# Latent tokens ordered by column in the neighbourhood attention, with scores for 416 keys instead of 512

## The chip, the cores and the metric

The kernel runs on one core of one Trainium2 chip. The metric is the device time of one execution in microseconds; the time of a kernel is the median of several runs. The core has TensorE (PE in the profile) with its weight loader (PEld), VectorE (DVE), ScalarE (ACT) and GpSimd (POOL); SyncE (SP) issues the transfers here.

## The reference, cut to what matters

Two layers of a backbone work on 256 latent and 256 context tokens of width 2048. Layer 0 mixes tokens by pooling, layer 1 by neighbourhood attention with 32 heads of 64; each is followed by a gated FFN of width 5504. Every sub-layer has an RMS norm, whose result is scaled and shifted by a modulation made from two vectors, one for each stream. The latent tokens are a grid of 4 rows and 64 columns. A latent query reads, in all 4 rows, the 16 columns around its own (clamped at the edges), with a learned bias by the distance in rows and columns, and beside these all 256 context keys:

```python
col_start = jnp.clip(col - kw // 2, 0, GRID_W - kw)
col_ok = (col[None, :] >= col_start[:, None]) & (col[None, :] < col_start[:, None] + kw)
...
s_loc = jnp.einsum('bhqd,bhkd->bhqk', q_r, k_band, preferred_element_type=f32) * scale + bias
s_loc = jnp.where(band_ok, s_loc, -jnp.inf)
s_ctx = jnp.einsum('bhqd,bhkd->bhqk', q_r, kc, preferred_element_type=f32) * scale
p = jax.nn.softmax(jnp.concatenate([s_loc, s_ctx], axis=-1), axis=-1).astype(v_band.dtype)
return (jnp.einsum('bhqk,bhkd->bhqd', p[..., :n_loc], v_band)
        + jnp.einsum('bhqk,bhkd->bhqd', p[..., n_loc:], vc))
```

## The kernel before, in words

Weights come from memory in pieces of 128 × 1024 fp32 (512 KB), loaded by `load` (L130) on SP. `split` makes two parts of each, a high one on ACT (L146) and a low one on DVE (L148), in a type that TensorE multiplies in one pass (f32r). A product of activations and weights is three products of parts: high with high, high with low, low with high. Tokens lie along the free side of a tile, features along the partitions.

The stages follow one another. Stage 0 makes the modulation of layer 0 on PE (`mod_pe`, tiles wm, products L182) and the pooling mixer (products pm, L563 to L565, with weights wp). FFN 0 follows; meanwhile DVE makes the modulation of layer 1, a piece at a time (`pair` and `single`, L242 to L265, tiles wm again), by a generator that the FFN's loop steps through. Then `normalise` makes the input of the attention: for each of 16 tiles of features and each stream one product on DVE (L401), the high part on ACT (L404) and the low part on DVE (L409), each 128 × 256, into the tile A. The attention is `_attention` (L1113 on): the first value products `_values` (L1108 to L1110), and then a pair of heads at a time. `kq_tile` makes keys of 512 tokens (L1173 to L1175) and queries of 256 (L1191, L1195); `rot` turns the latent ones by the rotary table rp (DVE L1146, L1148, L1149; POOL L1147). `attend` runs for the pair before, interleaved with `kq_tile` by `step`:

- `scores`, for each head and each block r of 128 queries: two products of 512 keys, those of the latent tokens first (L1221, L1222); the bias is added and the row's extreme found on DVE (L1231), the exponential on ACT (L1235), the scaling on DVE (L1236, L1237). The bias of a head is a strip of 128 × 384 (192 KB), loaded once a head (L1219) into the middle of a tile of zeros, and read at two places for the two blocks. A strip holds the bias of a query of one grid row for six grid rows, so one strip serves all grid rows by a shift.
- `turned`, for each head and block: four PE transposes of 128 × 128 (L1244) and one copy out of PSUM on DVE (L1245) into the tile pt.
- `finish`, for each pair: eight value products in plain fp32, four tiles of keys times two heads, 256 queries each (L1256), and a copy of the result on ACT (L1259).

A projection by wo (L1317), FFN 1 and the last norm follow.

Nobody writes the order of an engine's work out by hand: the program's scheduler places each instruction in the order of its engine by its own estimate of times, with a few calls for high priority. So a transfer that waits for nothing can stand much earlier in SP's queue than where the code calls for it. The transfers on SP take eight completion semaphores in turn, and each waits until the one eight places before it has landed.

Of the kernel before, what the change touches and what calls it, by code (L numbers as in the profile page):

```python
# [10 lines left out]
F32 = mybir.dt.float32  # L11
F32R = mybir.dt.float32r
AF = mybir.ActivationFunctionType
ALU = mybir.AluOpType
# [3 lines left out]
P = 128  # L18
D = 2048
KT = D // P  # L20
T = 256
F = 5504
NF = F // P
H = 32
W = 64
EPS = 1e-6
MASKED = -1.0e30
PAD = 8
POOL_WINDOWS = (2, 4, 8, 16)

# [28 lines left out]
def kernel(ctx: ExitStack, tc: tile.TileContext, xT, cxT, wmod, wg, wu, wd, wp,  # L59
                         wq, wv, wo, vec, cc, rope, inv, strips, out):  # L60
    nc = tc.nc
# [3 lines left out]
    ap0 = ctx.enter_context(tc.tile_pool(name="ap0", bufs=1))  # L65
# [27 lines left out]
    ident = main.tile([P, P], F32, name="ident")  # L93
# [5 lines left out]
    hl = main.tile([P, KT, T], F32, name="hl")  # L99
# [107 lines left out]
    def mod_pieces(pool):  # L207
# [28 lines left out]
        def pair(a):  # L236

            acc = sums_of(f"macc_{a}")
            for k in range(KT):
                w = staged(f"wm1_{a}_{k}").rearrange("p (c n) -> p c n", c=2)  # L240
                g, kk = divmod(k, 4)
                nc.sync.dma_start(w, wmod[1, a : a + 2, g, :, 512 * kk : 512 * kk + 512].rearrange("c p n -> p c n"))  # L242
                if k == 0:
                    nc.vector.tensor_scalar(acc, w, sc2[:, k, 0:1], None, op0=ALU.mult)
                else:
                    nc.vector.scalar_tensor_tensor(acc, w, sc2[:, k, 0:1], acc, op0=ALU.mult, op1=ALU.add)  # L246
                yield 1.0
            for c in range(2):
                fold(acc[:, c], a + c + 8, f"{a + c}")
# [75 lines left out]
    def M(l, which, k, s):  # L325
        return modT[l, which * 4 + k // 4][:, k % 4, s : s + 1]
# [66 lines left out]
    A = {}  # L393

    def normalise(l, which, h_of, streams, rstd, pool, ks=range(KT), keep=A):

        for k in ks:
            a = ap0.tile([P, 2, 2, T], F32R, tag=f"A{k}", name=f"A{k}_{l}_{which}")
            y = pool.tile([P, 2, T], F32, tag="t2", name=f"nrm{l}{which}{k}")
            for s in streams:  # L400
                nc.vector.scalar_tensor_tensor(y[:, s], h_of(s)[:, k, :], M(l, which + 1, k, s),  # L401
                                               rstd[s] if type(rstd) is list else rstd[:, T * s : T * s + T],
                                               op0=ALU.mult, op1=ALU.mult)
                nc.scalar.activation(a[:, 0, s, :], y[:, s], AF.Identity, bias=M(l, which, k, s))  # L404
# [4 lines left out]
                ins = nc.vector.scalar_tensor_tensor(a[:, 1, s, :], y[:, s], M(l, which, k, s),  # L409
                                                     a[:, 0, s, :].bitcast(F32), op0=ALU.add, op1=ALU.subtract)  # L410
            keep[k] = a
            if l == 1 and k == 1:
                hold[:] = [ins.ins]
# [2 lines left out]


    v_first = []
    with ExitStack() as ph0:
        p0 = ph0.enter_context(tc.tile_pool(name="p0", bufs=1, reuse_waits="tile"))  # L420
        f0 = ph0.enter_context(tc.tile_pool(name="f0", bufs=6, reuse_waits="tile"))
# [57 lines left out]
        with ExitStack() as phs:  # L479
# [19 lines left out]
            for j in range(2):  # L499
                t = st.tile([P, 2, WP], F32, bufs=1, name=f"pad{j}")  # L500
# [3 lines left out]
            for j in range(2):  # L504
                t = st.tile([P, 158], F32, bufs=1, name=f"sh{j}")
# [430 lines left out]

    tail = _attention(tc, ap0, bank, ld, A, M, hl, wq, wv, wo, rope, strips, ident, v_first)

    with ExitStack() as ph2:
        f1 = ph2.enter_context(tc.tile_pool(name="f1", bufs=8, reuse_waits="tile"))
# [140 lines left out]
        for j, (a, b) in enumerate(((0, 4), (4, 6), (6, 8), (8, 12), (12, 16))):  # L1083
            v = hl[:, a:b, :]
# [28 lines left out]
def _attention(tc, ap0, bank, ld, A, M, hl, wq, wv, wo, rope, strips, ident, v_first):  # L1113

    nc = tc.nc

# [6 lines left out]
    with ExitStack() as es:  # L1123
        op = es.enter_context(tc.tile_pool(name="op", bufs=1, reuse_waits="tile"))
        at = es.enter_context(tc.tile_pool(name="at", bufs=2, reuse_waits="tile"))
        rp = op.tile([P, 2, T], F32, name="rp")
        nc.sync.dma_start(rp, rope)

        sts = []
        for j in range(2):  # L1130
            t = op.tile([P, 10 * W], F32, name=f"strip{j}")
            nc.gpsimd.memset(t, 0.0)
            sts.append(t)

        qzs = []
        for j in range(2):
            t = op.tile([P, 2, T], F32R, name=f"qz{j}")
# [75 lines left out]
        def scores(m, b, r):  # L1213

            h = 2 * m + b
            ks, qd, qz = KEYS[m]
            strip = sts[b]
# [3 lines left out]
            nc.tensor.matmul(ps, qd[:, b, P * r : P * r + P], ks[:, b, :], start=True, stop=False)  # L1221
            nc.tensor.matmul(ps, qz[:, b, P * r : P * r + P], ks[:, b, :], start=False, stop=True)  # L1222
            if r == 0:
                bias = strip[:, 2 * W : 10 * W].rearrange("p (a t) -> p a t", a=2)
            else:
                a = strip[:, :]
                bias = bass.AP(a.tensor, a.offset, [a.ap[0], [6 * W, 2], [1, 4 * W]])

            sb = at.tile([P, 512], F32, tag="sb", bufs=3, name=f"sb{h}_{r}")
            nm = at.tile([P, 1], F32, tag="nm", name=f"nm{h}_{r}")  # L1230
            nc.vector.tensor_tensor_reduce(  # L1231
                out=sb.rearrange("p (a t) -> p a t", a=2), in0=ps.rearrange("p (a t) -> p a t", a=2),
                in1=bias, scale=-1.0, scalar=3.0e38, op0=ALU.add, op1=ALU.min, accum_out=nm)
# [3 lines left out]
            nc.vector.tensor_scalar(sb, sb, sm, None, op0=ALU.mult)  # L1237
            return sb, sm

        def turned(m, b, r, sb, pt):  # L1240

            pT = bank("d", f"pT{2 * m + b}_{r}")
            for j in range(4):
                nc.tensor.transpose(pT[:, P * j : P * j + P], sb[:, P * j : P * j + P], ident)  # L1244
            nc.vector.tensor_copy(pt[:, :, P * r : P * r + P], pT.rearrange("p (j q) -> p j q", j=4))  # L1245

        def attend(m, v, vc):

            pts = [None, None]

            def finish():
                po = bank("d", f"o{m}")
                for j in range(4):
                    for b in range(2):
                        c = vc + 64 * b
                        nc.tensor.matmul(po[64 * b : 64 * b + 64, :T], v[:, j, c : c + 64], pts[b][:, j, :],  # L1256
                                         start=(j == 0), stop=(j == 3), tile_position=(0, 64 * b))
                O[m] = op.tile([P, T], F32, name=f"O{m}")
                nc.scalar.copy(O[m], po[:, :T])  # L1259

            probs = {}
            for i in range(6):
                if i == 1 and ending:
                    ending.pop()()
                if 2 <= i:
                    b, r = divmod(i - 2, 2)
                    if r == 0:
                        pts[b] = at.tile([P, 4, T], F32, tag="pt", name=f"pt{2 * m + b}")
# [189 lines left out]
```

## Time and profile before

| | |
|---|---|
| runs | median 3055.77 us, 3055.04 to 3058.32, three runs |
| the profiled execution's own time | 3055.81 us |
| its span | 3054.0 us |
| mean granted clock of PE in it | 0.992 |
| instructions | 40391 |
| products and transposes on PE | 14846 |
| bytes moved | 568 MB, mean 186 GB/s |

Times in the profile count from the span's start. PE, DVE and so on stand ahead of a row's line number (L1244 is line 1244 of the kernel) and of its tile names (out<-in). A row with x8 holds eight instructions in a row. In a table of windows each engine has its busy time and its number of instructions, then come the clock that PE was granted, the share of time in which the 16 transfer engines were busy (a little over 1 when full), and GB/s. In the views of waits a row says which engine and line waited, for what, and then the total in us, the number of times and the longest. Products on PE overlap, so the pitch from start to start is what one costs.

### The profile page before, as it was taken

Reading aid. Unit: us, or ns where it says so; the run is one execution under the profiler, and the core shown is the slowest. Engines: PE = TensorE matmul, PEld = TensorE weight load, DVE = VectorE, ACT = ScalarE, POOL = GpSimd, SP = SyncE. Lnnn points to the kernel's source line nnn. Section 1 sums busy time; section 2 is a strip of 40 time slices with the busy share of each in tenths; the row PEclk is TensorE's granted clock in tenths of the full one; section 3 lists DMA queues with packets and bytes.
Section 4 is the critical chain, followed back from the end, with each engine's and each line's share of the span. In section 5 each row is a group of like instructions: output and inputs, shape, how many; then the busy total and the mean of one; then the engine's idle time right before and its main releaser. Section 6 shows DMA issues by size and latency. Waiting matters only on the chain.

```text
span 3054.0 us, 40391 instructions
## 1 busy us (share of the span) xinstructions
PE 2985.7 (98%) x14846; PEld 2399.9 (79%) x14846; DVE 2052.7 (67%) x2830; ACT 1351.5 (44%) x2205; POOL 835.2 (27%) x800
## 2 busy tenths in 40 slices
PE   6999999999999999999999999999999999999998
PEld 2565678887888888888887887887878888888887
DVE  4445887676776867687776656474767666666666
ACT  3333473323334233333334434343545665666665
POOL 1011310302214030231412000000002566566665
PEclk9999999999999999999999999999999999999999
DMA  9878635455765856675672333333355556655563
GB/s 374 328 279 323 211 101 173 160 173 165 248 196 178 260 179 216 208 239 180 214 233 83 122 104 114 99 107 105 112 160 180 187 183 193 192 186 185 183 197 113
DMA packets 183302, 568.07 MB, mean 186 GB/s; under 512 B 17856, under 2 KB 26560, under 8 KB 183104
## 3 DMA queue, kind: packets, MB, share of 16 engines
q1 hardware_dynamic: 183104, 565.49, 56.8%
q8 instruction: 117, 1.92, 0.3%
q14 instruction: 81, 0.66, 0.1%
HBM read 559.12 MB, written 6.29 MB: 185 GB/s over the span
## 4 chain that ended last, share of the span: by engine, by line
PE 89%; issue 4%; DVE 3%; DMA 2%; ACT 1%; POOL 1%; SPq 0%; DVEq 0%; ACTq 0%; POOLq 0%
PE g L991 5%; PE u L991 5%; PE d L875 5%; PE d L877 5%; PE d L876 5%; PE d L1041 4%; PE u L840 4%; PE u L839 4%; PE u L838 4%; PE g L840 4%; PE g L839 4%; PE g L838 4%; PE g L994 3%; PE u L994 3%; PE d L1045 2%
## 5 line engine op out<-in xcount | busy, mean ns | idle before, releaser
L896 POOL TENSOR_TENSOR hl<-hl,dy 128x256 f32<-128x256 f32 x144 | 140.2, 974 | 950.0 <-ACT dy L893 683.8
L1058 POOL TENSOR_TENSOR hl<-hl,dy 128x256 f32<-128x256 f32 x320 | 331.5, 1069 | 188.4 <-ACT dy L1056 186.1
L265 DVE SCALAR_TENSOR_TENSOR macc<-wm,sc,macc 128x512 f32<-128x512 f32 x360 | 261.5, 780 | 8.0 <-DMA wm<-wmod 8.0
L246 DVE SCALAR_TENSOR_TENSOR macc<-wm,sc,macc 128x1024 f32<-128x1024 f32 x120 | 161.4, 1345 | 67.2 <-DMA wm<-wmod 66.4
L893 ACT ACTIVATE dy<-d,modT 128x256 f32<-128x256 f32 x224 | 93.5, 470 | 144.9 <-PE d L877 143.0
L896 POOL TENSOR_TENSOR hc<-hc,dy 128x256 f32<-128x256 f32 x144 | 138.7, 963 | 0.0
L1056 ACT ACTIVATE dy<-d,modT 128x512 f32<-128x512 f32 x160 | 104.4, 683 | 43.0 <-PE d L1045 41.5
L182 PE MATMUL mod<-wm,sc 128*32 128x512 f32 x640 | 102.0, 617 | 21.5 <-DVE n1q L348 19.4
L1147 POOL TENSOR_TENSOR rk<-rk,rp 128x256 f32<-128x256 f32 x16 | 13.2, 827 | 366.1 <-DVE rk L1146 310.4
L148 DVE TENSOR_TENSOR wd_2l<-wd,wd_2h 128x1024 fp32r<-128x1024 f32 (+1 forms) x44 | 58.5, 1338 | 61.2 <-ACT wd_2h L146 61.1
L148 DVE TENSOR_TENSOR wd_3l<-wd,wd_3h 128x1024 fp32r<-128x1024 f32 (+1 forms) x44 | 53.3, 1233 | 60.1 <-ACT wd_3h L146 60.0
L463 ACT ACTIVATE sg<-g 128x512 f32<-128x512 f32 x43 | 27.3, 634 | 148.9 <-DVE g L460 148.8
L550 POOL TENSOR_TENSOR pf<-ws,inv 128x256 f32<-128x256 f32 x32 | 27.9, 893 | 204.2 <-DVE ws L542 131.1
L146 ACT CAST wd_0h<-wd 128x1024 fp32r<-128x1024 f32 (+1 forms) x44 | 45.3, 1031 | 81.2 <-PE g L839 51.0
L148 DVE TENSOR_TENSOR wd_1l<-wd,wd_1h 128x1024 fp32r<-128x1024 f32 (+1 forms) x44 | 55.3, 1260 | 32.3 <-ACT wd_1h L146 32.3
L1235 ACT ACTIVATE sb<-sb,nm 128x512 f32<-128x512 f32 x64 | 46.1, 721 | 63.5 <-DVE nm L1231 63.2
L148 DVE TENSOR_TENSOR wd_0l<-wd,wd_0h 128x1024 fp32r<-128x1024 f32 (+1 forms) x44 | 55.0, 1255 | 24.2 <-ACT wd_0h L146 24.2
L182 PEld LDWEIGHTS mod<-wm,sc 128*32 128x32 f32 x640 | 18.4, 109 | 65.9 <-issue 32.4
L146 ACT CAST wd_1h<-wd 128x1024 fp32r<-128x1024 f32 (+1 forms) x44 | 44.9, 1028 | 55.4 <-PE u L839 27.0
L875 PE MATMUL d<-act,wd_0h 128*128 128x512 f32 x172 | 67.4, 396 | 1.0 <-ACT dy L893 1.0
L875 PE MATMUL d<-act,wd_3h 128*128 128x512 f32 x172 | 68.2, 396 | 0.0
L876 PE MATMUL d<-act,wd_2h 128*128 128x512 f32 x172 | 68.1, 396 | 0.0
(1704 smaller groups left out, 9393.7 us busy)
## 6 DMA issues: line engine op xcount, KB each, us to landing
wm<-wmod SPq DMA_DIRECT2D x384, 512.0 KB, 6.0
wd<-wd SPq DMA_DIRECT2D x168, 512.0 KB, 4.4
wg<-wg SPq DMA_DIRECT2D x156, 512.0 KB, 4.6
wu<-wu SPq DMA_DIRECT2D x156, 512.0 KB, 4.6
wv<-wv SPq DMA_DIRECT2D x32, 512.0 KB, 3.9
wk<-wq SPq DMA_DIRECT2D x32, 512.0 KB, 4.0
wq<-wq SPq DMA_DIRECT2D x32, 512.0 KB, 3.7
wo<-wo SPq DMA_DIRECT2D x32, 512.0 KB, 4.5
```

The costliest lines, as they stand in the source:

```text
L148: eng.tensor_tensor(lo[:, :n], t[:, :n], hi[:, :n].bitcast(F32), op=ALU.subtract)
L246: nc.vector.scalar_tensor_tensor(acc, w, sc2[:, k, 0:1], acc, op0=ALU.mult, op1=ALU.add)
L265: nc.vector.scalar_tensor_tensor(acc[:, s], w, sc2[:, k, s : s + 1], acc[:, s], op0=ALU.mult, op1=ALU.add)
L838: nc.tensor.matmul(ps, hi[:, c : c + P], xh, start=(k == 0), stop=False)
L839: nc.tensor.matmul(ps, hi[:, c : c + P], xl, start=False, stop=False)
L840: nc.tensor.matmul(ps, lo[:, c : c + P], xh, start=False, stop=(k == KT - 1))
L875: nc.tensor.matmul(ps, hi[:, o : o + P], xh, start=(i == 0), stop=False)
L876: nc.tensor.matmul(ps, hi[:, o : o + P], xl, start=False, stop=False)
L896: nc.gpsimd.tensor_tensor(h_of(s)[:, k, :], h_of(s)[:, k, :], y[:, s], op=ALU.add)
L991: nc.tensor.matmul(ps, hi[:, c : c + P], flat(B[k]), start=(k == 0), stop=False)
L994: nc.tensor.matmul(ps[:, T:], lo[:, c : c + P], B[k][:, 0], start=False, stop=(k == KT - 1))
L1058: nc.gpsimd.tensor_tensor(hl[:, k, :], hl[:, k, :], y[:, q], op=ALU.add)
```

## The change

Within layer 1's attention the latent tokens are taken by column: token 4 c + r in place of 64 r + c for row r and column c. A block of 128 queries is then 32 columns of all four rows, and its windows lie in 40 columns, 160 latent keys: 0 to 159 for the first block, 96 to 255 for the second. With the 256 context keys that makes 416.

- `normalise` writes the latent half of layer 1's A by column, with a step of four elements on ACT and DVE; the rotary table is put in the same order by two POOL copies.
- The strips no longer fit a block. For each block and head the program makes a band of 128 × 160 in memory: `band_pieces` copies the parts of the strips from memory to memory, in 256 transfers on SP (64 steps of four heads), each of 32 × 4 runs of 160 bytes. `pair` takes a step at every second piece of modulation, and what is left goes ahead of the attention.
- `scores` loads a band (80 KB) for each head and block, and POOL copies it by column into the tile that is added. The second block has two products of 416 keys; the first has two of 160 and two of 256. All that follows works on 416.
- `turned` makes three PE transposes. The 32 × 32 corner that is left over is turned on DVE. The copy on DVE is 384 wide. The tiles pt are set to zero once and kept.
- `finish` makes the value products of the first and the last latent tile for 160 queries only; ACT copies the result back to row order.

```diff
+BAND = 160
+NK = BAND + T
...
+                if k % 2:
+                    next(moves, None)
                 yield 1.0
...
-                nc.scalar.activation(a[:, 0, s, :], y[:, s], AF.Identity, bias=M(l, which, k, s))
+                hi, lo, v = a[:, 0, s, :], a[:, 1, s, :], y[:, s]
+                if l == 1 and s == 0:
+                    hi, lo, v = by_column(hi), by_column(lo), v.rearrange("p (r c) -> p r c", c=W)
+                nc.scalar.activation(hi, v, AF.Identity, bias=M(l, which, k, s))
...
+    def band_pieces():
+
+        for hb in range(H // 4):
+            for q in range(2):
+                for r in range(4):
+                    rows = slice(W * (r % 2) + 32 * q, W * (r % 2) + 32 * q + 32)
+                    a = 2 - 2 * (r // 2)
+                    src = strips[4 * hb : 4 * hb + 4, rows, :].rearrange("h q (a c) -> h q a c", c=W)
+                    dst = band[q][hb].rearrange("h (q r) (a c) -> h q r a c", r=4, a=4)
+                    for h in range(4):
+                        nc.sync.dma_start(dst[h, :, r], src[h, :, a : a + 4, 24 * q : 24 * q + 40])
+                    yield
...
+def by_column(a):
+
+    return a.rearrange("p (c r) -> p r c", r=T // W)
...
+        pts = []
+        for j in range(2):
+            t = op.tile([P, 4, T], F32, name=f"pt{j}")
+            nc.gpsimd.memset(t, 0.0)
+            pts.append(t)
...
-            if r == 0:
-                nc.sync.dma_start(strip[:, : 6 * W], strips[h])
+            bias = sts[r]
+            rows = at.tile([P, 4, 40], F32, tag="rows", name=f"rows{h}_{r}")
+            nc.sync.dma_start(rows, band[r][h // 4][h % 4].rearrange("p (a c) -> p a c", a=4))
+            nc.gpsimd.tensor_copy(by_column(bias[:, :BAND]), rows)
             ps = bank("d", f"s{h}_{r}")
-            nc.tensor.matmul(ps, qd[:, b, P * r : P * r + P], ks[:, b, :], start=True, stop=False)
-            nc.tensor.matmul(ps, qz[:, b, P * r : P * r + P], ks[:, b, :], start=False, stop=True)
...
+            for o, c, n in ((0, 96, NK),) if r else ((0, 0, BAND), (BAND, T, T)):
+                for x in (qd, qz):
+                    nc.tensor.matmul(ps[:, o : o + n], x[:, b, P * r : P * r + P], ks[:, b, c : c + n],
+                                     start=x is qd, stop=x is qz)
...
-            for j in range(4):
-                nc.tensor.transpose(pT[:, P * j : P * j + P], sb[:, P * j : P * j + P], ident)
-            nc.vector.tensor_copy(pt[:, :, P * r : P * r + P], pT.rearrange("p (j q) -> p j q", j=4))
+            for j, c in enumerate((BAND, BAND + P, 32) if r else (0, BAND, BAND + P)):
+                nc.tensor.transpose(pT[:, P * j : P * j + P], sb[:, c : c + P], ident)
+            nc.vector.tensor_copy(pt[:, r : r + 3, P * r : P * r + P], pT[:, : 3 * P].rearrange("p (j q) -> p j q", j=3))
+            if r:
+                nc.vector.transpose(pt[96:128, 0, 128:160], sb[0:32, 0:32])
+            else:
+                nc.vector.transpose(pt[0:32, 3, 96:128], sb[96:128, 128:160])
...
-                for j in range(4):
+                for j, i, q in ((1, 2, slice(0, T)), (2, 3, slice(0, T)), (0, 0, slice(0, BAND)), (3, 1, slice(T - BAND, T))):
                     for b in range(2):
...
-                nc.scalar.copy(O[m], po[:, :T])
+                nc.scalar.copy(O[m].rearrange("p (r c) -> p r c", c=W), by_column(po[:, :T]))
```

The order of the instructions changes with it at the places below. A row has its line in the kernel that it belongs to (the new kernel's lines are a little further down), and a tile's number is only its own.

On SP, in stage 0, before: the loads of the modulation (wm_0_2, wm_0_3: its last pieces for the first block; wm_8: the next block) and of the pooling weights wp follow one another.

```order
L130 DMA wm_0_2_1024_312<-wmod 128x1024
L130 DMA wm_0_3_0_318<-wmod 128x1024
L130 DMA wm_0_3_1024_320<-wmod 128x1024
L130 DMA wp_0_328<-wp 128x1024
L130 DMA wp_1024_330<-wp 128x1024
L130 DMA wm_8_0_0_349<-wmod 128x1024
L130 DMA wm_8_0_1024_351<-wmod 128x1024
```

After, at the same place, L439 being the copies of the bands:

```order
L132 DMA wm_0_3_0_336<-wmod 128x1024
L439 DMA band_0_89<-strips 32x4x40 x9
L132 DMA wm_0_3_1024_338<-wmod 128x1024
L132 DMA wp_0_346<-wp 128x1024
L439 DMA band_0_89<-strips 32x4x40 x7
L132 DMA wp_1024_348<-wp 128x1024
L132 DMA wm_8_0_0_367<-wmod 128x1024
L439 DMA band_0_97<-strips 32x4x40
L132 DMA wm_8_0_1024_369<-wmod 128x1024
```

All 256 copies stand within the first 246 places of SP's queue counted by rows (a row can hold several), that is in stage 0 and not in FFN 0, where the code calls for them; the loads keep their order among themselves.

On PE, in the attention, before: the two score products stand among the key products of the next pair.

```order
L1174 MATMUL k_14191<-A_1_0_13109,wk4h_14175 128x512
L1221 MATMUL s_0_14317<-ks_13833,qd_13890 128x512
L1222 MATMUL s_0_14317<-ks_13833,qz_13200 128x512
L1175 MATMUL k_14191<-A_1_0_13109,wk4l_14176 128x512
L1173 MATMUL k_14191<-A_1_0_13117,wk4h_14175 128x512
```

After, for a first block (s_0), with the transposes of blocks before it:

```order
L1281 MATMUL pT_0_14107<-ident,sb_0_14057 128x128 x3
L1213 MATMUL k_14030<-A_1_0_13391,wk3h_14014 128x512
L1264 MATMUL s_0_14163<-ks_13914,qd_13975 128x160
L1264 MATMUL s_0_14163<-ks_13914,qz_13479 128x160
L1264 MATMUL s_0_14163<-ks_13914,qd_13975 128x256
L1264 MATMUL s_0_14163<-ks_13914,qz_13479 128x256
L1214 MATMUL k_14030<-A_1_0_13391,wk3h_14014 128x512
```

Two products of 512 became four shorter ones, and three transposes stand where there were four.

On POOL, in the attention, after; before, the rope products (rk and rq) followed one another with nothing between:

```order
L1260 COPY bias_13473<-rows_1_13993 128x4x40
L1260 COPY bias_13471<-rows_0_14049 128x4x40
L1187 TENSOR_TENSOR rk_13909<-rk_13909,rp 128x256
L1260 COPY bias_13473<-rows_1_14082 128x4x40
L1187 TENSOR_TENSOR rq_13970<-rq_13970,rp 128x256
```

The bias copies, two for each head, now stand between them.

More of the change, by code (lines that the diff above doesn't have):

```diff
@@ L418 @@
     v_first = []
+    dram = ctx.enter_context(tc.tile_pool(name="dram", bufs=1, space=bass.MemoryType.DRAM))
+    band = [[dram.tile([4, P, BAND], F32, name=f"band{q}_{hb}") for hb in range(H // 4)] for q in range(2)]
+    def band_pieces():
[9 more added lines that the diff above has]
+                    yield
+    moves = band_pieces()
     with ExitStack() as ph0:
@@ L935 @@
         hold.clear()
-    tail = _attention(tc, ap0, bank, ld, A, M, hl, wq, wv, wo, rope, strips, ident, v_first)
+    for _ in moves:
+        pass
+    tail = _attention(tc, ap0, bank, ld, A, M, hl, wq, wv, wo, rope, band, ident, v_first)
     with ExitStack() as ph2:
@@ L1110, in _values, with _attention @@
                 nc.tensor.matmul(pv[i], xl, hi[:, c : c + 512], start=False, stop=(k == KT - 1))
-def _attention(tc, ap0, bank, ld, A, M, hl, wq, wv, wo, rope, strips, ident, v_first):
+def _attention(tc, ap0, bank, ld, A, M, hl, wq, wv, wo, rope, band, ident, v_first):
     nc = tc.nc
@@ L1126, in _attention @@
         rp = op.tile([P, 2, T], F32, name="rp")
[L1127 removed]
+        raw = at.tile([P, 2, T], F32, tag="sb", bufs=3, name="rope_rows")
+        nc.sync.dma_start(raw, rope)
+        for j in range(2):
+            nc.gpsimd.tensor_copy(by_column(rp[:, j, :]), raw[:, j, :].rearrange("p (r c) -> p r c", c=W))
         sts = []
         for j in range(2):
[L1131 removed]
+            t = op.tile([P, NK], F32, name=f"bias{j}")
             nc.gpsimd.memset(t, 0.0)
             sts.append(t)
+        pts = []
+        for j in range(2):
+            t = op.tile([P, 4, T], F32, name=f"pt{j}")
+            nc.gpsimd.memset(t, 0.0)
+            pts.append(t)
         qzs = []
```

22 lines of the change are left out of this document (6 added, 16 removed).

## The prediction

> **What bounds the kernel now.** The page comes first: which engine is full, and how full the transfers are.
>
> ```profile
> span 3054.0 us, 40391 instructions
> PE 2985.7 (98%) x14846; PEld 2399.9 (79%) x14846; DVE 2052.7 (67%) x2830; ACT 1351.5 (44%) x2205; POOL 835.2 (27%) x800
> q1 hardware_dynamic: 183104, 565.49, 56.8%
> ```
>
> TensorE is busy for 98% of the span, but this is an average over stages. So the second view is the table of windows: the start of stage 0, its middle, its end, and the inside of the attention; then two windows in which the transfers are full, with rows of 1 KB (352) and of 4 KB (120); then the two sides of the normalisation ahead of the attention.
>
> ```profile
> core 0: us, PE busy (x) PEld busy (x) DVE busy (x) ACT busy (x) POOL busy (x), PEclk, DMA share, GB/s
> 8.00:45.00 37.00, 20.85 (x98) 5.72 (x98) 23.88 (x45) 17.68 (x45) 7.46 (x9) 0.97 1.03 410
> 45.00:85.00 40.00, 33.71 (x152) 17.85 (x150) 17.17 (x38) 11.37 (x21) 3.38 (x4) 0.85 0.95 365
> 85.00:250.00 165.00, 163.47 (x902) 96.42 (x899) 82.46 (x133) 55.60 (x96) 21.73 (x25) 1.00 0.84 312
> 1700.00:2200.00 500.00, 500.00 (x2491) 403.10 (x2490) 298.35 (x584) 214.79 (x373) 26.35 (x31) 1.00 0.35 109
> ```
> ```profile
> 352.00:358.00 6.00, 4.73 (x27) 3.63 (x26) 3.34 (x10) 1.04 (x1) 1.02 (x1) 1.00 1.01 359
> 120.00:140.00 20.00, 20.00 (x100) 10.03 (x94) 12.16 (x24) 7.20 (x13) 3.10 (x4) 1.00 1.03 407
> ```
> ```profile
> 1670.00:1695.00 25.00, 25.00 (x102) 20.20 (x101) 25.00 (x57) 14.79 (x31) 1.98 (x4) 0.91 0.17 63
> ```
>
> The stages have two different limits. In the attention PE is busy for 500.00 of 500 us with transfers at 0.35: each nanosecond of PE time saved there is saved from the span. At the start the transfers are full (1.03) and PE is busy for 20.85 of 37 us: there what counts is when a load lands. The waits of PE around the attention confirm the first half; the columns are us in total, times, longest.
>
> ```profile
> PE o L1256 <- DVE pt L1245: 1.9, 2, 1.7
> PE n3b L377 <- DVE n3d L375: 1.9, 1, 1.9
> PE pT L1244 <- DVE sb L1237: 1.2, 1, 1.2
> ```
>
> The longest sum is 1.9 us, so shorter softmax work on DVE and ACT brings next to nothing by itself. All sums below stand against the profiled execution's own 3055.8 us, which equals the median of the runs (3055.77).
>
> **The attention.** The timeline of PE inside it gives the prices, as the pitch from one start to the next (the listed durations overlap).
>
> ```profile
> 1903.27 1.11 PE L1195 MATMUL q<-A,wq6l 128*128 128x256 f32 x8
> 1904.31 1.95 PE L1256 MATMUL o<-pt,vt 128*64 128x256 f32 x16
> 1906.19 0.50 PE L1173 MATMUL k<-A,wk7h 128*128 128x512 f32 x1
> ...
> 1913.22 0.60 PE L1244 MATMUL pT<-ident,sb 128*128 128x128 f32 x4
> 1913.58 0.47 PE L1173 MATMUL k<-A,wk7h 128*128 128x512 f32 x1
> 1913.90 0.39 PE L1174 MATMUL k<-A,wk7h 128*128 128x512 f32 x1
> ...
> 1918.46 0.40 PE L1221 MATMUL s<-ks,qd 128*128 128x512 f32 x1
> 1918.70 0.40 PE L1222 MATMUL s<-ks,qz 128*128 128x512 f32 x1
> 1918.93 0.40 PE L1174 MATMUL k<-A,wk7h 128*128 128x512 f32 x1
> ```
>
> A product of 512 columns costs 0.23 us (1918.70 to 1918.93). Eight of 256 take 1.04 us (1903.27 to 1904.31), 0.13 each. The line through both is 0.03 us plus 0.39 ns a column.
>
> Transposes: four of them and one key product take 1913.90 − 1913.22 = 0.68 us; less 0.23 leaves 0.45, so 0.11 each. There are 32 heads × 2 query blocks, so 64 go: −7.0 us.
>
> Value products: 1906.19 − 1904.31 = 1.88 us for a head pair's eight, 0.235 each. Four of the eight shrink from 256 to 160 queries. Proportional, that saves 0.235 × 96/256 = 0.088; with the fixed 0.03 it is 0.077. 0.077 × 4 × 16 pairs = −4.9 us (ends 0 and −5.6).
>
> Scores, second block: two products of 416 in place of two of 512: 96 × 0.39 ns × 2 × 32 = −2.4 us.
>
> Scores, first block: its keys are 0 to 159 and 256 to 511, so two products become four (160, 160, 256, 256). The 256 costs 0.13. No product of this type narrower than 256 stands in the trace. The line gives 0.09 for 160, hence 2 × (0.09 + 0.13) = 0.44 against 0.46, −0.6 us in all. The other end is the price of the value products, which run on plain f32: two of them, side by side in the two halves of the array, take 0.47 us for 256 columns, (0.47 − 0.03)/256 = 1.7 ns a column, 0.30 for 160; then 2 × (0.30 + 0.13) = 0.86, +0.40 × 32 = +13 us. I take 0.11, the transposes' price, nearest in width: 2 × (0.11 + 0.13) = 0.48, +0.6 us.
>
> Sum in the attention: −7.0 − 4.9 − 2.4 + 0.6 = −13.7 us.
>
> Nothing there for the rest. DVE is busy for 298 of 500 us and gets shorter copies, plus one 32×32 transpose per block; ACT (215 of 500) copies O with a stride; the strip loads become twice as many and smaller, with transfers at 0.35. POOL, 26 of 500 us, gets 64 bias copies ahead of the rope products in its queue, and before the attention two zero fills and two reorderings of the rope table:
>
> ```profile
> L1147 POOL TENSOR_TENSOR rk<-rk,rp x16: 731/828/921, 1728.8 to 2193.8; 128x256 f32<-128x256 f32 x16
> ```
>
> The first rope product starts only at 1728.8, 30 us into the stage, which covers the fills (some 2 us each as estimated from 828 ns for 256 elements). Without that cover, each late microsecond would stand in the path of the first scores.
>
> **The normalisation.** Its latent half is now written with a step of four elements, 16 writes on DVE and 16 on ACT. DVE is full there (25.00 of 25 us), so DVE time is span.
>
> ```profile
> L409 DVE SCALAR_TENSOR_TENSOR A<-nrm,modT,A x32: 479/488/496, 1670.9 to 1697.8; 128x256 fp32r<-128x256 f32 x32
> ```
>
> No write with a step stands in the trace. Free, it costs 0; at twice the time, 16 × 0.49 = +7.8 us. I take +0.8, a tenth of the time, nearer to the row as it stands, because the 32 forms there keep within 17 ns of each other (479 to 496) whatever their stream. The Trainium skill (Advanced Engine Details and Errata, Memory Cachelines) says that SBUF has lines of 16 bytes and that an access to a new line each time pays a penalty, and a step of four fp32 is just that. By it the term would go toward its upper end. No run here shows which.
>
> **The 256 band copies.** They are called for from the loader of layer 1's modulation, but the order places them in stage 0, among its loads, in SP's queue. There the issue is what is scarce:
>
> ```profile
> 9.97 18.69 SPq L130 DMA_DIRECT2D wm<-wmod  x16
> 29.59 1.61 SPq L130 DMA_DIRECT2D wp<-wp  x2
> 32.15 13.53 SPq L130 DMA_DIRECT2D wm<-wmod  x11
> ```
> ```profile
> SPq L130 <- DMA wm<-wmod: 26.4, 28, 2.0
> ```
> ```profile
> SPq L130 <- PE mod L182: 120.1, 50, 11.3
> ```
>
> Transfers on SP share eight completion semaphores in turn, so each waits until the one eight places before it has landed; that is the 26.4 us of waits for wm in the first 60 us, one every 1.2 us (18.69/16). In the first 300 us it also waits 120.1 us for PE to free buffers. Nine bands now stand ahead of the load wm_0_3_1024, the sixteenth of the first row, which went out at about 28. Each takes a place that a landed load frees, 9 × 1.2 = 10 us later: issue at about 38. Its landing then takes about the 3.9 us of a lone 512 KB load:
>
> ```profile
> strip<-strips SPq DMA_DIRECT2D x32, 192.0 KB, 2.6
> wv<-wv SPq DMA_DIRECT2D x32, 512.0 KB, 3.9
> ```
> ```profile
> 38.53 1.05 PE L182 MATMUL mod<-wm,sc 128*32 128x512 f32 x4 [0.24 <-DMA wm<-wmod]
> ```
> ```profile
> 29.59 8.59 DMA wp<-wp
> ...
> 47.13 2.07 PE pm L563 x4
> ```
>
> So it lands at 42, where PE used it at 38.53: +3.5. The chain of waits to the first pooling product (47.13) goes through wp instead, and the modulation has some slack beside it; seven more bands stand ahead of the second half of wp. I put +2 on pm.
>
> What a band costs the transfers: it is 128 runs of 160 B, 8 for each of 16 transfer engines. Full transfers of 4 KB rows move 407 GB/s at a share of 1.03, so 395 at 1; 4096 × 16/395 = 166 ns a row. For 1 KB, 359/1.01 gives 355, 46 ns. The line is 6 ns plus 0.039 ns a byte; at 160 B 12 ns, 0.1 us a band. The strip (1536 B rows, 192 KB in 2.6 us) against wv (3.9) has a smaller slope, and by it a run has some 25 ns in it: 0.25 us a band. Ends: 0.05 (20.5 KB at 410 GB/s) and 1.2 (8 times the mean packet, 0.568 × 3054 × 16/183104 = 0.15 us). I take 0.1 to 0.12, nearest to the row of short writes. Some 53 bands fall into 45 to 85 us, where 5% of 40 us is idle: 53 × 0.1 − 2 = +3.3. The other 187 fall into 85 to 250, 16% of 165 = 26 us idle: 19 to 22 us fit, but the loads behind them wait for their eight places; +2.7, half of what a longest wait of 11.3 us leaves uncovered at 0.12. Together +8 us (ends +1 and +30).
>
> The Trainium skill (DMA: Bandwidth & Descriptors, Specifications) speaks against this: a transfer reaches line rate only from 512 B up, below which the engine reads, modifies and writes. By that a band would move its bytes two or three times, an estimate of 0.10 to 0.15 us, and the term would be +8 to +13. No transfer in the trace is this short.
>
> **Sum.** −13.7 + 0.8 + 8 = −4.9 us: 3055.8 − 4.9 = 3050.9, rounded 3051.
>
> **The rivals.**
>
> *The bands are hidden altogether* (0.05 to 0.08 us each, and the slack of 4 to 14 us covers the start): −13.7 + 0.8 = −12.9, 3043 us. For it: total idle transfer time in stage 0 is 28 us. Against: the start has none. Chance 0.15.
>
> *The short runs are dear, and it ends slower.* At 0.25 us a band: 3.5 at the start, 53 × 0.25 − 2 = 11, 187 × 0.25 − 26 = 21, less the 5 us that loads stand ahead of PE: +30, hence 3055.8 − 12.9 + 30 = 3073. The gain in the attention is used up when the bands cost 13 us, about 0.16 us each; from there it decides. For it: no row so short, SP busy waiting already; against: the 1 KB row. Chance 0.26.
>
> *The 160-column products run at the price of f32*, +13 in place of +0.6: 3063 us. For it: the trace shows the one-pass price at 256 and 512 columns only. Against: the line through these has hardly a fixed part. Chance 0.22; with dear bands as well it is 3085.
>
> *The strided writes take twice as long*: +7.8 in place of +0.8, 3058 us. For it: DVE has no idle time in that window; against: no row. Chance 0.04. The Trainium skill's rule on lines of 16 bytes, above, is on its side.
>
> *POOL's queue*: a bias copy waits for a late row load and holds the rope product behind it, half a product (0.4 us) in each of 16 pairs: +6.6, 3058 us. Against: POOL is busy for a twentieth of that time. Chance 0.03.
>
> The forecast keeps 0.30.
>
> **How the numbers follow.** The runs spread by about 0.1%, so 0.2%, 6 us, is what a measurement tells from no change: under 3049.7 is faster, over 3061.9 slower. Faster: the hidden bands (0.15) and the lower two fifths of the forecast's case (0.12), 0.27. Same: the rest of it (0.18), the f32 price with cheaper bands (0.09), strided writes and POOL (0.07), 0.34. Slower: dear bands (0.26) and most of the f32 case (0.13), 0.39. Slower is thus the likeliest of the three signs, though 3051 is the likeliest single case; its own range is 3044 to 3058. The range that holds 8 in 10 reaches from 3042 (bands hidden) to 3080 (dear bands, one step short of the dear products too).
>
> **What would show it.** In the new profile, the attention should be 13 to 14 us shorter, with PE still full; a pitch of 0.11 for the 160-column products is right, 0.30 is the f32 rival. The first pm should start near 49 (47.13 now) and the waits of PE for wm in the first 250 us should grow by some 6 us; 30 us is the dear rival, none the hidden one. The prediction is wrong if stage 0 ends as early as now, or if PE waits for POOL or DVE inside the attention.

## The result and the profile after

The changed kernel takes 3122.55 us (median of five, 3120.37 to 3124.02) against 3055.04 us (3054.38 to 3058.32): 1.0218 times as long, 95% interval 1.0203 to 1.0233. It is 67.5 us slower; the forecast was 3051 and the range ended at 3080.

Where the time went shows at the starts of the first products of each stage, in us of the span, read from the two traces:

| first product | before | after | later by |
|---|---|---|---|
| pm (pooling, L563 / L587) | 47.1 | 53.8 | 6.7 |
| cg (first FFN product, in stage 0) | 77.6 | 92.4 | 14.8 |
| g (FFN 0 proper) | 406.5 | 485.5 | 79.0 |
| modt_b (end of layer 1's modulation) | 1621.4 | 1700.8 | 79.4 |
| v (values of the attention) | 1668.4 | 1748.0 | 79.6 |
| k (keys) | 1715.1 | 1795.0 | 79.9 |
| op (projection after the attention) | 2200.3 | 2267.1 | 66.8 |
| end of the span | 3054.0 | 3120.4 | 66.4 |

So stage 0 lost 79 us, FFN 0 and the normalisation about one, and the attention gave back 13.

The table of windows of the changed kernel, for the same stretches of stage 0 that the prediction shows of before:

```profile
45.00:85.00 40.00, 28.81 (x120) 12.51 (x120) 12.52 (x26) 8.33 (x12) 1.71 (x2) 0.80 0.87 273
85.00:250.00 165.00, 133.04 (x636) 68.26 (x631) 54.02 (x95) 45.90 (x85) 12.98 (x18) 0.89 0.76 241
```

PE was busy for 163.47 of 165 us from 85 to 250, and is now for 133.04. But the transfers did not fill up, though every version of the prediction had more work for them in the same time: their share fell from 0.84 to 0.76, and the rate from 312 to 241 GB/s. PE waits for loads that are not on their way. The next view is what PE waited for in the first 400 us, before and then after:

```profile
PE mod L182 <- DVE n1q L348: 19.4, 1, 19.4
...
PE mod L182 <- DMA wm<-wmod: 1.4, 6, 0.2
```
```profile
PE mod L184 <- DMA wm<-wmod: 68.8, 20, 20.3
PE modt L196 <- ACT modev L191: 4.4, 6, 0.8
```

The longest wait of each (19.4 and 20.3 us) is the one before PE's very first product, so it is not new. The rest of the waits for wm went from 1.4 to 48.5 us. That is not the whole loss. From 20 us to the start of FFN 0 proper PE runs the same 1969 products in both kernels:

```profile
20.00:406.50 386.50, 366.38 (x1969) 217.12 (x1965) 226.19 (x377) 145.62 (x269) 77.03 (x83) 0.98 0.79 289
```
```profile
20.00:485.50 465.50, 401.30 (x1969) 219.13 (x1969) 225.05 (x378) 146.15 (x270) 75.87 (x83) 0.94 0.76 252
```

PE's idle time grows from 20.1 to 64.2 us, 44 of the 79. The other 35 us are busy time for the same products, with a mean granted clock of 0.94 where it was 0.98. How much of the 35 us the clock explains was not separated.

And now SP, which sends them. The waits of SP between 45 and 180 us, of before and then of after; here PE is the engine that frees a buffer, and a DMA the load that held one of the eight places:

```profile
SPq L130 <- PE mod L182: 59.5, 23, 11.3
SPq L130 <- DMA wm<-wmod: 22.9, 23, 2.3
SPq L130 <- PE cu L719: 6.8, 3, 6.2
SPq L130 <- PE pw L673: 3.1, 1, 3.1
SPq L130 <- DMA wcg<-wg: 3.0, 3, 1.6
...
SPq L130 <- DMA wcu<-wu: 1.9, 2, 0.9
```
```profile
SPq L439 <- DMA wm<-wmod: 19.0, 22, 2.1
SPq L132 <- DMA wm<-wmod: 3.4, 5, 0.9
SPq L132 <- PE mod L184: 1.9, 5, 0.5
SPq L132 <- DMA wcg<-wg: 1.2, 2, 0.6
SPq L595 <- DMA wm<-wmod: 1.0, 1, 1.0
SPq L439 <- DMA wcg<-wg: 0.9, 1, 0.9
SPq L132 <- DMA wcu<-wu: 0.8, 1, 0.8
```

Before, SP waited for PE for 59.5 + 6.8 + 3.1 = 69.4 us of these 135: it had time to spare, all buffers were full. After, 1.9 us. The waits for places hardly differ (27.8 and 26.3 us in these rows). What fills the difference is SP's own time to issue; the rows give the shortest, median and longest issue in ns, of the copies and then of the loads wm in the same window (the loads' last line of before for comparison):

```profile
L439 SPq DMA_DIRECT2D band<-strips x112: 550/598/1421, 46.0 to 179.6; - x112
```
```profile
L132 SPq DMA_DIRECT2D wm<-wmod x50: 327/410/1129, 45.6 to 162.4; - x50
```
```profile
L130 SPq DMA_DIRECT2D wm<-wmod x64: 327/340/577, 45.3 to 176.2; - x64
```

112 copies at 0.6 us are 67 us. With all loads (62 where there were 80 before, in all 28 us) and the places (26) and the waits for PE (2) that is 124 of 135 us; the rest lies between instructions. SP is full, and the order is fixed, so a load goes out when the copies ahead of it have been issued. A stretch of SP's timeline shows ten copies between two loads:

```profile
113.06 0.54 SPq L132 DMA_DIRECT2D wcu<-wu  x1
113.64 6.68 SPq L439 DMA_DIRECT2D band<-strips  x10
120.42 1.01 SPq L132 DMA_DIRECT2D wm<-wmod  x2
```

The chain of waits that ended last goes, around that place, mostly through loads on their way and PE's products behind them:

```profile
110.03 5.21 DMA wcu<-wu
...
124.58 7.66 DMA wm<-wmod
132.70 7.32 DMA wm<-wmod
140.07 3.13 PE mod L184 x13
143.19 5.08 DMA wm<-wmod
```

### The profile page after: what moved, and what is told of

It reads as the page before. It is cut to its first block, busy times and chain, and to the rows that moved or that the text cites. A ratio compares the mean times of both kernels' runs of the same rounds, so it can differ in the third digit from the quotient of the medians.

```text
span 3120.4 us, 40893 instructions
## 1 busy us (share of the span) xinstructions
PE 3006.9 (96%) x14846; PEld 2401.3 (77%) x14846; DVE 2045.9 (66%) x2894; ACT 1346.9 (43%) x2205; POOL 875.7 (28%) x868
## 4 chain that ended last, share of the span: by engine, by line
PE 87%; DMA 5%; issue 3%; DVE 2%; ACT 1%; POOL 1%; SPq 1%; DVEq 0%; ACTq 0%; POOLq 0%
PE g L1017 5%; PE u L1017 5%; PE d L899 5%; PE d L901 5%; PE d L900 5%; PE d L1067 4%; PE u L864 4%; PE u L862 4%; PE u L863 4%; PE g L864 4%; PE g L862 4%; PE g L863 4%; DMA wm<-wmod 3%; PE u L1020 3%; PE g L1020 3%
## 5 line engine op out<-in xcount | busy, mean ns | idle before, releaser
L184 PE MATMUL mod<-wm,sc 128*32 128x512 f32 x640 | 129.0, 657 | 69.8 <-DMA wm<-wmod 68.8
L1260 POOL COPY bias<-rows 128x160 f32<-128x160 f32 x64 | 37.4, 587 | 306.3 <-issue 189.0
L184 PEld LDWEIGHTS mod<-wm,sc 128*32 128x32 f32 x640 | 20.8, 113 | 129.8 <-DMA wm<-wmod 64.2
L901 PE MATMUL d<-act,wd_0l 128*128 128x512 f32 x172 | 67.9, 395 | 0.0
```

The source lines that it names most:

```text
L901: nc.tensor.matmul(ps, lo[:, o : o + P], xh, start=False, stop=(i == n - 1))
```

## The experiments

The theory, S: each of the 256 copies holds SP for about 0.6 us in stage 0, and so the loads behind it, which PE needs, are late. Rivals: T, the transfer engines are held by the short runs; L, the copies take places among the eight semaphores; R, the scheduler's other order is to blame. Each run names what it leaves out.

**The copies later.** The copies stay, in the same queue, but go where the code calls for them:

```diff
-                nc.sync.dma_start(w, wmod[1, a : a + 2, g, ...
+                at = nc.sync.dma_start(w, wmod[1, a : a + 2, g, ...
...
                 if k % 2:
-                    next(moves, None)
+                    with tc.issue_after(at.ins):
+                        next(moves, None)
```

> The changed kernel with one edit: each group of four band copies is queued on SP right behind the modulation load of layer 1 beside which the code calls for it (about 770 to 1590 us of the span), not in stage 0. Nothing is left out. Theory S (the 256 copies cost SP's queue in stage 0 about 0.6 us each, and the loads behind them land late): stage 0 ends as before, the gain of 12.9 us in the attention stays, 3043 us, at most +5 where a copy delays a load of FFN 0. Rival T (short runs are dear for the transfer engines wherever they stand): some 50 us of transfer time collide with FFN 0's loads instead, 3060 to 3100 us. Rival R (the loss comes from elsewhere, for instance the order that the scheduler now finds): stays near 3122.

Measured 3046.85 us (3039.71 to 3047.21, six runs), ratio to before 0.9967 (0.9955 to 0.9980). The same 256 copies take as long to issue there:

```profile
L440 SPq DMA_DIRECT2D band<-strips x256: 550/599/1727, 780.4 to 1595.3; - x128
```

Between 770 and 1600 us SP waits for DVE to free the buffers of layer 1's modulation; the longest sums of before are these:

```profile
SPq L242 <- DVE macc L246: 122.0, 96, 2.3
SPq L257 <- DVE macc L265: 74.1, 35, 4.2
```

The 154 us of issue fit into them, and PE does not notice: no wait of PE for a load in FFN 0. S holds, T and R fall: the copies' transfers, and the rest of the new order, cost next to nothing there. L is not tested by this run, since a place that is held matters as little there as an issue.

**No copies in memory, direct loads in the attention.**

```diff
-            nc.sync.dma_start(rows, band[r][h // 4][h % 4].rearrange("p (a c) -> p a c", a=4))
+            for g in range(4):
+                src = band[h, W * (g % 2) + 32 * r : W * (g % 2) + 32 * r + 32, :].rearrange("q (a c) -> q a c", c=W)
+                a = 2 - 2 * (g // 2)
+                nc.sync.dma_start(rows[g::4], src[:, a : a + 4, 24 * r : 24 * r + 40])
```

Here `band` is the argument's name and holds the strips; `band_pieces` is not called.

> No bands in memory: each tile of 128 x 160 is loaded from the strips in the attention by four transfers of 32 x 4 runs of 160 bytes, 256 in all, on SP. Nothing is left out. Theory S: SP has 500 us there and issues little, 256 x 0.6 = 154 us fit, stage 0 is as before: 3043 us, up to 3050 if weight loads behind the bursts of four come late. Rival T: no better than the copies elsewhere, 3060 or more. A rival of its own: the bias comes late and POOL's copy holds the rope products, +7 to +15.

Measured 3042.62 us (3037.85 to 3044.69, four runs), ratio 0.9960 (0.9945 to 0.9974): the lowest median of the kernels that compute all, though its runs overlap with those of the kernel with late copies. An issue is as long as that of a copy:

```profile
L1262 SPq DMA_DIRECT2D rows<-strips x256: 598/603/1652, 1697.6 to 2199.4; - x128
```

POOL's copies waited 11.2 us for rows in all, PE for nothing of this. So it is not the short runs, nor the number of issues in itself, but the stage in which they stand in SP's queue.

**The copies issued by GpSimd.** `nc.sync` becomes `nc.gpsimd` at L439.

> The changed kernel with the 256 copies issued by GpSimd instead of SP, still in stage 0, with completion semaphores of their own. The same runs and bytes move at about the same time. Nothing is left out. Theory S (SP's issue and its queue): SP's loads come as before, most of the 79 us of stage 0 goes, unless GpSimd's own work in stage 0 is held by the issuing: 3045 to 3075. Rival T (transfer time of the runs): stage 0 stays some 70 us longer, 3110 to 3122.

Measured 3076.95 us (3075.99 to 3078.36), ratio 1.0075 (1.0060 to 1.0090). Of the 67 us 46 are gone, with the same bytes in stage 0. This run does not speak against T by itself, because the runs are not the same: in its trace a copy is 16 packets of 1280 bytes (4096 in all), where it is 128 of 160 from SP's queue (32,768). SP waits for PE again between 45 and 180 us:

```profile
SPq L132 <- PE mod L184: 54.8, 17, 14.3
SPq L132 <- DMA wm<-wmod: 30.0, 30, 1.9
```

What remains against the kernel with late copies (30 us) goes with GpSimd being held by the copies, as far as the trace shows: in the first 45 us it is busy for 34.19 us (10.87 in the changed kernel), in which its own issues count (0.552 us each in the median), and the first pooling product pm starts at 63.2 instead of 53.8. That this is all of the 30 us was not tested.

```profile
0.00:45.00 45.00, 19.54 (x86) 6.87 (x86) 13.33 (x29) 15.24 (x38) 34.19 (x70) 1.00 0.96 369
```

**Longer runs, same bytes.** Each copy takes 32 runs of 640 bytes from one place; the bias is that of other places.

```diff
-                        nc.sync.dma_start(dst[h, :, r], src[h, :, a : a + 4, 24 * q : 24 * q + 40])
+                        nc.sync.dma_start(band[q][hb][h, 32 * r : 32 * r + 32], strips[4 * hb + h, rows, :BAND])
```

> The changed kernel with the 256 copies in the same number and bytes, but each of 32 runs of 640 bytes instead of 128 of 160. It leaves out the reordering: the bias that is added is that of other places. Theory S with the issue time set by the number of runs (0.6 us for 128 on both sides, 0.33 for 32): 256 x 0.27 = 69 us of SP's time go, stage 0 loses about half of its 79 us or more, 3065 to 3095. Theory S with the issue time set by the number of transfers: near 3115. Rival L (places among the eight semaphores, whatever the issue takes): 3110 to 3122. Rival T: a run of 640 bytes takes 32 ns against 4 x 14, so 24 of 31 us stay on a full transfer engine, 3110.

Measured 3109.53 us (3105.17 to 3115.86), ratio 1.0182 (1.0167 to 1.0198). A quarter of the runs saves 13 us, not 60: the issue hardly gets shorter, 588 ns in the median against 599. The form of S in which the issue's length follows the number of runs falls. The other form (near 3115), L (from 3110) and T (3110) all lie close to the measured time, so this run does not tell them apart; T is decided by the two last runs below.

**Half of the copies late.** The first 128 stay in stage 0, the others go to FFN 0.

```diff
-                    with tc.issue_after(at.ins):
+                    with tc.issue_after(at.ins) if a >= 16 else ExitStack():
```

> The changed kernel with the first 128 copies left in stage 0 and the other 128 queued in FFN 0 as in the run with all of them late. Nothing is left out. In the profile of before SP stood about 200 us of stage 0 waiting for PE to free buffers; after, 33. Theory S (SP's queue is full): 128 copies need about 77 us of issue and as much again in slower issues and places, within those 200, so only the start (+7 to +15 until cg) is paid: 3050 to 3062. A rival in which each copy costs the same wherever it stands in stage 0 (79/256 = 0.31 us): half of 79, 3082 to 3086.

Measured 3083.50 us (3081.02 to 3086.12), ratio 1.0093 (1.0078 to 1.0108). This is the rival's number, and my form of S, in which SP's idle time anywhere in stage 0 could take in the copies, was wrong. The waits of SP in this run, from 45 to 180 us and from 180 to 340, say why:

```profile
SPq L440 <- DMA wm<-wmod: 21.1, 28, 2.0
SPq L132 <- DMA wm<-wmod: 4.5, 6, 1.4
SPq L132 <- PE mod L184: 2.2, 5, 0.5
```
```profile
SPq L132 <- PE mod L184: 61.2, 31, 7.6
SPq L132 <- DMA wm<-wmod: 25.8, 27, 3.2
```

The scheduler does not spread the copies; it packs the 128 into the first 175 us, and as long as they last SP is as full as with 256 (2.2 us of waits for PE). After them it waits for PE as before, but that time is no longer of use: PE is full again (78.87 of 80 us from 250 to 330) and cannot catch up. So a copy cost some 0.3 us wherever it stood in a stretch in which SP was full: (3083.50 − 3041.86)/128 = 0.33 here, against the run without copies below, and 79/256 = 0.31 with all of them.

**The kernel before with the copies alone.** Nothing else of the change, and nothing reads the bands.

```diff
+    moves = band_pieces()
...
+                if k % 2:
+                    next(moves, None)
```

> The kernel before with nothing changed but the 256 copies added, which its scheduler places in stage 0; nothing reads them. Theory S: the 79 us of stage 0 come whole and nothing else changes, 3130 to 3137 us. If the order that the scheduler finds for the rest had a part in it, the time lies clearly under that, for instance 3100.

Measured 3136.43 us (3134.29 to 3138.42), ratio 1.0269 (1.0252 to 1.0286): 81.4 us over its own before (3055.00). The copies are the whole loss, and the two parts of the change add up: 81.4 − 67.5 = 13.9 us that the rest of it gains. R falls.

**The copies issued by ACT.** `nc.sync` becomes `nc.scalar` at L439; the copies still take their places among the same eight semaphores. In the trace they are again 128 packets of 160 bytes each.

> The changed kernel with the 256 copies issued by ACT in stage 0. They share the eight completion semaphores with SP's loads, in turn, unlike GpSimd's. Nothing is left out. Theory S (SP's time to issue is what counts): near the run with GpSimd's queue, 3060 to 3090, ACT's own work being held 0.6 us by each copy. Rival L (the places among the eight): no better than the changed kernel, 3110 to 3130.

Measured 3106.07 us (3103.28 to 3110.21), ratio 1.0168 (1.0153 to 1.0183), between the expectations of both and a little under the rival's. SP no longer issues the copies, yet it waits for places, from 45 to 180 us:

```profile
SPq L132 <- DMA wm<-wmod: 50.6, 33, 4.6
SPq L132 <- DMA band<-strips: 39.9, 17, 7.5
SPq L132 <- PE mod L184: 13.5, 14, 5.1
```

That is 90 us where it was 26; with GpSimd's queue, whose copies have semaphores of their own, it is 30.0. So SP is now held by the places. But PE is hardly held by that. Its waits in the first 420 us:

```profile
PE modt L196 <- ACT modev L191: 26.1, 6, 10.0
PE mod L184 <- DMA wm<-wmod: 21.4, 2, 20.9
PE mod L184 <- ACT modev L191: 15.0, 2, 8.8
```

Of the waits for wm 20.9 us are again the one before the first product; 0.5 us are left, where the changed kernel had 48.5. PE waits for ACT's copy modev (L191) instead, 41.1 us against 5.1, and ACT has the copies' issues ahead of it. So with the issues off SP the loads are in time for PE, although the places are still taken; this speaks for S and against L. The two are not fully parted: with PE held by ACT a late load shows less, and how much of the 106 − 77 = 29 us between the runs on ACT's and on GpSimd's queue is the places was not tested.

**No copies at all.** Each tile of 128 × 160 is one load from the strips, in runs of 640 bytes; the bias is that of other places.

> The changed kernel without copies: each tile of 128 x 160 is one contiguous load from the strips. It leaves out the bands, so that the bias that is added is that of other places. What is left is the change without its price: by the landmarks 3055.8 + 0.3 - 12.9 = 3043 us for both theories. If it is as high as the run with direct loads (3042.6) or higher, the 256 short loads in the attention cost nothing.

Measured 3041.86 us (3036.14 to 3045.67), ratio 0.9955 (0.9941 to 0.9970): as by the landmarks, and as much as with direct loads (3042.62), so these cost nothing that can be told.

**The copies an eighth as large, and the copies flat.** To the run without copies, 256 transfers are put back at the same places of SP's queue. One kernel moves 16 runs of 160 bytes in each, the other the whole 20 KB in 16 runs of 1280. Nothing reads them, and the bias is that of other places.

```diff
-                        nc.sync.dma_start(dst[h, :, r], src[h, :, a : a + 4, 24 * q : 24 * q + 40])
+                        nc.sync.dma_start(band[q][hb][h, 16 * r : 16 * r + 16, :40], strips[4 * hb + h, 16 * r : 16 * r + 16, :40])
```

> The run without copies (3041.9), with 256 transfers from memory to memory put back at the same places of SP's queue in stage 0, each of only 16 runs of 160 bytes, one for each transfer engine (2.5 KB instead of 20). Nothing reads them, and the bias is left out of order as in the run without copies. Theory S (SP's time per issue): if an issue still takes 0.5 to 0.6 us, the time is again some 60 to 79 us up, 3100 to 3121; if it takes 0.33, about half of that, 3065 to 3085. Rival T (bytes and runs): an eighth of the transfer time is left, 3042 to 3055.

> As the run before, but each of the 256 transfers moves the full 20 KB, in 16 runs of 1280 bytes. Nothing reads them, and the bias is left out of order. Theory S: the same time as with 2.5 KB, within 10 us, since only the number of issues and their length count. Rival T: 8 times the bytes in runs of 1280 are some 0.06 us a transfer on every engine, 15 us over the tiny ones.

Measured 3112.86 us (3110.78 to 3114.14), ratio 1.0185 (1.0170 to 1.0200), with 2.5 KB, and 3109.49 us (3108.21 to 3112.14), ratio 1.0173 (1.0157 to 1.0190), with 20 KB. With an eighth of the bytes the loss is still 71 of 81 us (3112.86 and 3122.55, each less 3041.86). This is the clearest of the runs: what counts is not what a copy moves. The tiny copies take as many issues and as many places as the large ones, so these two runs do not part S from L. The issue of the tiny copies from 45 to 180 us:

```profile
L439 SPq DMA_DIRECT2D band<-strips x108: 488/582/1467, 44.8 to 179.1; - x108
```

T falls for nearly all of it; the 10 to 13 us between these runs (and the one with longer runs) and the changed kernel are what the form of 32 × 4 × 40 adds, in issue (550 against 488 ns at the shortest) or transfer; the runs do not tell which.

## Why the prediction was wrong, point by point

**The step that failed** is "What a band costs the transfers". It priced a band by the time of the transfer engines, 0.1 to 0.12 us, and let 187 of them "fit" into 26 us of idle transfer time. The price was right: in the trace's packet records, the 29,610 packets of 160 bytes between 45 and 330 us took 14 ns in the median, where the line through two windows gave 12. But the transfer engines were not what was scarce. The time in which SP issues was not counted at all, though the prediction had written that the issue is what is scarce there, and counted nine places for the first load only. At 0.6 us, 256 issues are 154 us; stage 0 became 79 us longer instead of 8. The waits of SP for PE, 120.1 us in the first 300, were quoted, but only the longest of them, 11.3 us, went into the sum: together they were the whole spare time of that queue.

**Terms that do not come out of their lines.** The +2.7 us for the bands after 85 us can't be worked out as it is described: 187 × 0.12 less 11.3 leaves 11.1 us, and half of that is 5.6. The 25 ns of a run, by the strip against wv, don't follow either: the two loads (2.6 and 3.9 us, 8 rows for an engine) give 0.063 ns a byte, a steeper line than 0.039 and not a flatter one, and 25 ns × 8 would be 0.20 us a band, not 0.25. Neither changes which step failed.

**The rival "dear"** had the right sign and place, and its price a band (0.25 us; 79/256 = 0.31) was near by luck: the price had no line behind it, the mechanism was wrong, and the idle transfer time that it took off as cover was no cover. The prediction gave "slower" 0.39, more than the other two signs, but by way of dear runs and the f32 price, neither of which decided. The Trainium skill (DMA: Bandwidth & Descriptors, Specifications) says that a transfer gets line rate only from 512 B up, and that the engine reads, modifies and writes below it. This did not decide the time: runs of 1280 bytes lost 68 us, runs of 160 bytes 71 to 81. In rate the trace does show short packets worse, 160 B in 14 ns against 4096 in 159, 11 against 26 bytes a ns for one engine.

**The start.** pm came at 53.8, forecast near 49; the nine copies ahead of wm_0_3_1024 were issued from 29.08 to 39.27, so the load went out at 39.38, against 38 forecast.

**The attention.** Forecast −13.7, measured −12.9 from the first value product to the first projection; 13.9 by the kernel with the copies alone. PE was full as forecast (487.00 of 487 us from 1780 to 2267). Two of its parts, by the timeline of PE; first the value products of a pair:

```profile
1959.59 1.62 PE L1295 MATMUL o<-pt,vt 128*64 128x256 f32 x14
1961.14 0.50 PE L1213 MATMUL k<-A,wk6h 128*128 128x512 f32 x1
```

They take 1961.14 − 1959.59 = 1.55 us: −0.33 × 16 = −5.3 (forecast −4.9). Then the four products of a first block, at a place where no transpose stands beside them:

```profile
1927.39 0.23 PE L1264 MATMUL s<-ks,qd 128*128 128x160 f32 x1
1927.47 0.28 PE L1264 MATMUL s<-ks,qz 128*128 128x160 f32 x1
1927.58 0.32 PE L1264 MATMUL s<-ks,qd 128*128 128x256 f32 x1
1927.73 0.28 PE L1264 MATMUL s<-ks,qz 128*128 128x256 f32 x1
1927.85 0.40 PE L1213 MATMUL k<-A,wk4h 128*128 128x512 f32 x1
```

They take 1927.85 − 1927.39 = 0.46 us, as much as the two products of before (0.46): 0 (forecast +0.6). The two of 160 columns take 1927.58 − 1927.39 = 0.19 us together, 0.09 to 0.10 each and not 0.30: the f32 rival falls, and the line's 0.09 for 160 columns was nearer than the 0.11 that the forecast took.

**The normalisation.** The strided writes take longer: in the trace 16 of the 32 on DVE take 661 to 707 ns and the other 16 465 to 474, and on ACT 16 take 709 to 772 and the others 462 to 513. The Trainium skill (Advanced Engine Details and Errata, Memory Cachelines) speaks of a penalty where each access goes to another line of 16 bytes. The trace agrees.

```profile
L416 DVE SCALAR_TENSOR_TENSOR A<-nrm,modT,A x32: 465/568/707, 1750.3 to 1780.5; 128x256 fp32r<-128x256 f32 x32
```

That is 0.2 us each, 3.4 us of DVE time, where the forecast took 0.05 us each. But from modt_b to the first key product the span grew by 0.5 us only: most of it was not on the path, though DVE was full in the window (25.00 of 25 us from 1750).

**POOL's queue.** No wait of PE for POOL stands among its waits in the attention (the longest sum there is 1.9 us, for DVE); this rival falls.

## What to carry to other kernels

A transfer had three prices here: the time of the engines that move it, the place that it holds until it has landed, and the time that the issuing queue takes to send it. When many small transfers are added to a queue that feeds a stage limited by loads, count issues first, by the row of the issue, against that queue's own idle time in the same stretch, and look in the order where the scheduler really puts them: here one line that ties the copies to a later stage turned 67 us lost into 8 us won (0.9967, interval 0.9955 to 0.9980). A saving in a full stage is what its pitches say; it is worth the more to leave out the preparation altogether, as the direct loads do.

## What the runs showed of the hardware

The issue of a transfer on SP took 0.327 us at the shortest for a load of 128 rows (wm), 0.488 for copies from memory to memory of 16 or 32 runs (0.58 to 0.59 in the median), and 0.55 to 0.60 for 32 × 4 × 40, from memory to memory or into the chip alike. An eighth of the bytes, in the same 16 runs, did not shorten it. Between 45 and 180 us the loads wm among the copies took 410 ns in the median (340 before). The runs do not separate what in the pattern sets these lengths.

The same 32 × 4 × 40 copy was 128 packets of 160 bytes in the trace when SP or ACT issued it, and 16 packets of 1280 bytes when GpSimd did.
